# Attention on one core: probabilities as the stationary operand of the second matmul, in an order written by hand

## The chip, the cores and the metric

One NeuronCore of a Trainium2 chip runs the whole kernel. The metric is the device time of one execution in microseconds (us), the median over runs. TensorE does the matmuls and transposes (its weight loads, PEld, overlap them), ScalarE (ACT) the exponentials, VectorE (DVE) copies and arithmetic, GpSimd (POOL) casts and fills, SyncE (SP) issues transfers.

## The reference

```python
# q, k, v: (8, 8, 512, 64) float32: batch, heads, sequence, dim
scores = einsum('bhqd,bhkd->bhqk', q, k) / sqrt(64)
scores = scores - scores.max(axis=-1, keepdims=True)
attn = exp(scores)
attn = attn / attn.sum(axis=-1, keepdims=True)
return einsum('bhqk,bhkd->bhqd', attn, v)
```

There are 64 heads, each with a 512 x 512 matrix of scores. Neither kernel subtracts the maximum: both take the exponential of the scaled scores as they are and divide at the end by the sum over the keys.

## The kernel before

Heads are taken in 32 pairs, four to a batch entry. The 512 rows of a head lie on the 128 partitions four to a partition, so that a partition's four rows are neighbours in memory; chunk i (of `NI` = 4) is the i-th row of every partition. One pair goes through these stages.

- **Loads.** GpSimd's queue loads q and k of a batch entry at a time (`batch_load`, L49 and L54) and v head by head (L77), and the transfers turn fp32 into fp16 on their way. v lies in `vp` with a 65th column of ones (L75), so that the second matmul also gives the sum of the exponentials.
- **Transposes of q and k.** VectorE places the two heads of the pair side by side in `qkp` (L84, L88). TensorE transposes the eight 128 x 128 blocks into one bank of PSUM (L95, L96), and VectorE copies them out as `tqk` (L98). Head A then has its 64 dims on partitions 0 to 63, head B on 64 to 127.
- **Scores.** A matmul of 64 rows gives 128 keys (on partitions) by 512 queries (L110). A score tile holds two key chunks of one head, 128 x 1024 in fp32, two banks; there are two such tiles. ScalarE takes the exponential of a whole tile into fp16 `pt` (L118): four per pair, 128 in all.
- **Second matmul.** v with its ones is the stationary operand (128 x 65), 512 columns of `pt` stream past it, and four chunks add up into `ot`, 65 x 512: dims and sum on partitions, queries along the row (L131).
- **Output.** VectorE copies `ot` to SBUF (L140), TensorE transposes it back in four blocks per head, in fp32 (L148), and VectorE takes the reciprocal of the sum (L153) and multiplies (L154). SyncE stores 256 KB per pair (L161).

The order on each engine is the scheduler's of the tile framework: it interleaves the stages of neighbouring pairs by its own priorities, so the order in the text below is not the order on an engine. Buffers of a pool go round (`bufs`), and an instruction that writes one waits for the last reader of its former content.

Of the kernel before, what the change touches and what calls it, by code (L numbers as in the profile page):

```python
# [8 lines left out]
FP32 = mybir.dt.float32  # L9
FP16 = mybir.dt.float16  # L10

EXP = mybir.ActivationFunctionType.Exp
# [3 lines left out]
@with_exitstack  # L16
def kernel(
    ctx: ExitStack,
    tc: tile.TileContext,
    q: bass.AP,  # L20
    k: bass.AP,
    v: bass.AP,
    out: bass.AP,
):
    nc = tc.nc
    B, H, S, D = q.shape
    P = 128
    NI = S // P
    assert NI == 4 and D == 64 and S == 512
    scale = float(D) ** -0.5  # L30

    n_pairs = (B * H) // 2
    ppb = H // 2

    cpool = ctx.enter_context(tc.tile_pool(name="att_const", bufs=1))
    bpool = ctx.enter_context(tc.tile_pool(name="att_batch", bufs=2))
    apool = ctx.enter_context(tc.tile_pool(name="att_a", bufs=4))
    ppool = ctx.enter_context(tc.tile_pool(name="att_pair", bufs=3))
    hpool = ctx.enter_context(tc.tile_pool(name="att_head", bufs=4))
    opool = ctx.enter_context(tc.tile_pool(name="att_out", bufs=3))  # L40
    pspool = ctx.enter_context(tc.tile_pool(name="att_psum", bufs=1, space=bass.MemoryType.PSUM))

    bt = {}
    ident16 = None
    ident32 = None

    def batch_load(b):
        q16 = bpool.tile([P, H, NI * D], FP16, tag="q16", name=f"q16_{b}")
        nc.gpsimd.dma_start(  # L49
            out=q16.rearrange("p h (i d) -> p h i d", d=D),  # L50
            in_=q[b].rearrange("h (p i) d -> p h i d", i=NI),
        )
        k16 = bpool.tile([P, H, NI * D], FP16, tag="k16", name=f"k16_{b}")
        nc.gpsimd.dma_start(  # L54
            out=k16.rearrange("p h (i d) -> p h i d", d=D),
            in_=k[b].rearrange("h (p i) d -> p h i d", i=NI),
        )
        bt[b] = (q16, k16)

    batch_load(0)  # L60
    ident16 = cpool.tile([P, P], FP16, name="ident16")
    make_identity(nc, ident16)
    ident32 = cpool.tile([P, P], FP32, name="ident32")
    make_identity(nc, ident32)

    for g in range(n_pairs):
        b = g // ppb
        gl = g % ppb
        hA = 2 * gl
        if gl == 0 and b + 1 < B:  # L70
            batch_load(b + 1)
        q16, k16 = bt[b]

        vp = apool.tile([P, 2, NI, D + 1], FP16, tag="vp", name=f"vp_{g}")
        nc.gpsimd.memset(vp[:, :, :, D : D + 1], 1.0)  # L75
        for h01 in range(2):
            nc.gpsimd.dma_start(  # L77
                out=vp[:, h01, :, 0:D],
                in_=v[b, hA + h01].rearrange("(p i) d -> p i d", i=NI),
            )  # L80

        qkp = apool.tile([P, 2, NI, P], FP16, tag="qkp", name=f"qkp_{g}")
        for h01 in range(2):
            nc.vector.tensor_copy(  # L84
                out=qkp[:, 0, :, 64 * h01 : 64 * h01 + 64],
                in_=q16[:, hA + h01, :].rearrange("p (i d) -> p i d", d=D),
            )
            nc.vector.tensor_copy(  # L88
                out=qkp[:, 1, :, 64 * h01 : 64 * h01 + 64],
                in_=k16[:, hA + h01, :].rearrange("p (i d) -> p i d", d=D),  # L90
            )

        tqk_ps = pspool.tile([P, 2, NI, P], FP16, tag="ps_tqk", bufs=1, name=f"tqkps_{g}")
        for i in range(NI):
            nc.tensor.transpose(tqk_ps[:, 0, i, :], qkp[:, 0, i, :], ident16)  # L95
            nc.tensor.transpose(tqk_ps[:, 1, i, :], qkp[:, 1, i, :], ident16)  # L96
        tqk = ppool.tile([P, 2, S], FP16, tag="tqk", name=f"tqk_{g}")
        nc.vector.tensor_copy(out=tqk[:, :, :], in_=tqk_ps[:, :, :, :])  # L98

        pt = [hpool.tile([P, NI, S], FP16, tag="pt", name=f"pt_{g}_{h}") for h in range(2)]  # L100
        for half in range(2):
            st_ps = [
                pspool.tile([P, 2, S], FP32, tag="ps_st", bufs=2, name=f"st_{g}_{h01}_{half}")
                for h01 in range(2)
            ]
            for cc in range(2):
                c = 2 * half + cc
                for h01 in range(2):
                    po = 64 * h01
                    nc.tensor.matmul(  # L110
                        st_ps[h01][:, cc, :],
                        tqk[po : po + 64, 1, c * P : (c + 1) * P],
                        tqk[po : po + 64, 0, :],
                        start=True,
                        stop=True,
                    )
            for h01 in range(2):
                nc.scalar.activation(  # L118
                    out=pt[h01][:, 2 * half : 2 * half + 2, :],
                    in_=st_ps[h01][:, :, :],  # L120
                    func=EXP,
                    scale=scale,
                )

        ot_ps = [
            pspool.tile([P, S], FP32, tag="ps_ot", bufs=2, name=f"ot_{g}_{h01}")
            for h01 in range(2)
        ]
        for h01 in range(2):
            for c in range(NI):  # L130
                nc.tensor.matmul(  # L131
                    ot_ps[h01][0 : D + 1, :],
                    vp[:, h01, c, :],
                    pt[h01][:, c, :],
                    start=(c == 0),
                    stop=(c == NI - 1),
                )
        ot_sb = opool.tile([P, 2, S], FP32, tag="ot_sb", name=f"otsb_{g}")
        for h01 in range(2):
            nc.vector.tensor_copy(out=ot_sb[0 : D + 1, h01, :], in_=ot_ps[h01][0 : D + 1, :])  # L140

        out_sb = opool.tile([P, 2, NI, D], FP32, tag="out_sb", name=f"outsb_{g}")
        rcp = opool.tile([P, 2, NI], FP32, tag="rcp", name=f"rcp_{g}")
        for h01 in range(2):
            op_ps = pspool.tile([P, NI, D + 1], FP32, tag="ps_outp", bufs=1,
                                name=f"outp_{g}_{h01}")
            for c in range(NI):
                nc.tensor.transpose(  # L148
                    op_ps[:, c, :],
                    ot_sb[0 : D + 1, h01, c * P : (c + 1) * P],  # L150
                    ident32[0 : D + 1, 0 : D + 1],
                )
            nc.vector.reciprocal(out=rcp[:, h01, :], in_=op_ps[:, :, D : D + 1])  # L153
            nc.vector.tensor_tensor(  # L154
                out=out_sb[:, h01, :, :],
                in0=op_ps[:, :, 0:D],
                in1=rcp[:, h01, :].broadcast_to([P, NI, D]),
                op=AluOp.mult,
            )

        nc.sync.dma_start(  # L161
            out=out[b, hA : hA + 2].rearrange("h (p i) d -> p h (i d)", i=NI),
            in_=out_sb[:, :, :, :],
        )


# [28 lines left out]
```

## Time and profile before

| | |
|---|---|
| time, median of 3 runs | 191.35 us (190.75 to 191.9) |
| span of the profiled execution, its own time from the first to the last instruction | 189.0 us |
| TensorE matmul busy | 166.8 us (88%), 1024 instructions |
| ScalarE busy | 125.2 us (66%) |
| VectorE busy | 115.1 us (61%) |
| GpSimd busy | 66.5 us (35%) |
| granted TensorE clock, mean | 0.998 |
| HBM read, written | 25.17 MB, 8.39 MB |

The span is what the profiler saw of one execution; the median is of other executions of the same kernel, 2.35 us longer. A matmul's busy time counts the whole of its way through the array, so matmuls that follow each other overlap, and a busy TensorE is not one at its peak.

### The profile page before, as it was taken

Reading aid. Unit: us, or ns where it says so; the run is one execution under the profiler, and the core shown is the slowest. Engines: PE = TensorE matmul, PEld = TensorE weight load, DVE = VectorE, ACT = ScalarE, POOL = GpSimd, SP = SyncE. Lnnn points to the kernel's source line nnn. Section 1 sums busy time; section 2 is a strip of 40 time slices with the busy share of each in tenths; the row PEclk is TensorE's granted clock in tenths of the full one; section 3 lists DMA queues with packets and bytes.
Section 4 is the critical chain, followed back from the end, with each engine's and each line's share of the span. In section 5 each row is a group of like instructions: output and inputs, shape, how many; then the busy total and the mean of one; then the engine's idle time right before and its main releaser. Section 6 shows DMA issues by size and latency. Waiting matters only on the chain.

```text
span 189.0 us, 2952 instructions
## 1 busy us (share of the span) xinstructions
PE 166.8 (88%) x1024; PEld 74.9 (40%) x1024; DVE 115.1 (61%) x352; ACT 125.2 (66%) x129; POOL 66.5 (35%) x120
## 2 busy tenths in 40 slices
PE   0057999999999999999999999999999999999980
PEld 0033433434444343544353443434353443434330
DVE  0255455675859486666759585766757594656462
ACT  2014388688786868686886868686877868686860
POOL 7482643423453335413543336304133333300000
PEclk9999999999999999999999999999999999999999
DMA  3999999965599578995699478996555463631111
GB/s 42 191 182 183 129 156 189 179 87 77 65 147 196 80 91 111 182 170 83 86 143 188 74 91 126 179 149 87 83 83 76 34 90 67 87 69 59 55 57 55
DMA packets 59150, 21.16 MB, mean 112 GB/s; under 512 B 34560, under 2 KB 59136, under 8 KB 59136
## 3 DMA queue, kind: packets, MB, share of 16 engines
q0 software_dynamic: 50432, 12.59, 70.2%
q1 hardware_dynamic: 8704, 8.39, 12.8%
q8 instruction: 8, 0.13, 0.3%
q14 instruction: 6, 0.05, 0.1%
HBM read 25.17 MB, written 8.39 MB: 178 GB/s over the span
## 4 chain that ended last, share of the span: by engine, by line
PE 68%; DVE 11%; ACT 9%; DMA 6%; issue 2%; POOL 2%; ACTq 1%; POOLq 0%
PE st L110 31%; PE ot L131 31%; ACT pt L118 9%; DMA k<-in_k_dram 6%; DVE otsb L140 5%; DVE tqk L98 5%; PE outp L148 4%; PE tqkps L95 1%; POOL q L49 1%; ACTq L190 0%; POOL k L54 0%; DVE outsb L154 0%; DVE qkp L88 0%; POOL ident masks.py:199 0%; PE tqkps L96 0%
## 5 line engine op out<-in xcount | busy, mean ns | idle before, releaser
L118 ACT ACTIVATE pt<-st 128x1024 f16<-128x1024 f32 x128 | 124.0, 1024 | 56.8 <-PE st L110 56.8
L131 PE MATMUL ot<-pt,vp 128*65 128x512 f16 x256 | 73.4, 390 | 0.3 <-ACT pt L118 0.3
L140 DVE COPY otsb<-ot 65x512 f32<-65x512 f32 x64 | 43.8, 685 | 43.5 <-PE ot L131 43.5
L110 PE MATMUL st<-tqk 64*128 64x512 f16 x256 | 65.6, 386 | 3.6 <-DVE tqk L98 0.8
L77 POOL DMA_DIRECT2D vp<-in_v_dram x64 | 47.2, 743 | 14.4 <-POOL vp L75 9.6
L131 PEld LDWEIGHTS <-vp 128*65 128x65 f16 x256 | 21.9, 111 | 41.5 <-issue 33.9
L148 PEld LDWEIGHTS outp<-ident,otsb 65*128 65x128 f32 x256 | 23.4, 141 | 17.8 <-DVE otsb L140 9.3
L148 PE MATMUL outp<-ident,otsb 65*128 65x65 f32 x256 | 27.4, 229 | 3.2 <-DVE outsb L154 1.4
L75 POOL MEMSET vp<- 128x8 f16 x32 | 4.0, 139 | 70.6 <-PE ot L131 70.6
L95 PE MATMUL tqkps<-ident,qkp 128*128 128x128 f16 x128 | 21.0, 231 | 8.7 <-DVE qkp L84 7.6
L154 DVE TENSOR_TENSOR outsb<-outp,rcp 128x256 f32<-128x256 f32 x64 | 27.0, 422 | 1.3
L110 PEld LDWEIGHTS <-tqk 64*128 64x128 f16 x256 | 13.3, 94 | 25.7 <-issue 16.6
L96 PE MATMUL tqkps<-ident,qkp 128*128 128x128 f16 x128 | 20.9, 230 | 2.8 <-DVE qkp L88 2.8
L98 DVE COPY tqk<-tqkps 128x1024 f16<-128x1024 f16 x32 | 21.4, 670 | 0.5 <-PE tqkps L96 0.5
L84 DVE COPY qkp<-q 128x256 f16<-128x256 f16 x64 | 15.6, 256 | 8.4 <-DMA q<-in_q_dram 8.4
L153 DVE RECIPROCAL rcp<-outp 128x4 f32<-128x4 f32 x64 | 11.2, 175 | 14.5 <-PE outp L148 14.2
L95 PEld LDWEIGHTS <-qkp 128*128 128x128 f16 x128 | 12.8, 102 | 18.3 <-issue 7.6
L88 DVE COPY qkp<-k 128x256 f16<-128x256 f16 x64 | 16.4, 275 | 2.7 <-DMA k<-in_k_dram 2.7
L96 PEld LDWEIGHTS <-qkp 128*128 128x128 f16 x128 | 13.2, 103 | 6.9 <-DVE qkp L88 2.9
L49 POOL DMA_DIRECT2D q<-in_q_dram x8 | 7.2, 902 | 12.6 <-DVE qkp L88 9.2
L54 POOL DMA_DIRECT2D k<-in_k_dram x8 | 7.1, 892 | 0.1
L118 ACT ACT_TABLE_LOAD x1 | 1.3, 1283 | 0.7 <-PEq L179 0.7
(6 smaller groups left out, 1.3 us busy)
## 6 DMA issues: line engine op xcount, KB each, us to landing
out_dram<-outsb SPq DMA_DIRECT2D x32, 256.0 KB, 2.4
q<-in_q_dram POOLq DMA_DIRECT2D x8, 512.0 KB, 6.6
k<-in_k_dram POOLq DMA_DIRECT2D x8, 512.0 KB, 8.2
vp<-in_v_dram POOLq DMA_DIRECT2D x64, 64.0 KB, 3.1
```

What stands on the lines that cost most here:

```text
L77: nc.gpsimd.dma_start(out=vp[:, h01, :, 0:D], in_=v[b, hA + h01].rearrange("(p i) d -> p i d", i=NI),)
L84: nc.vector.tensor_copy(out=qkp[:, 0, :, 64 * h01 : 64 * h01 + 64], in_=q16[:, hA + h01, :].rearrange("p (i d) -> p i d", d=D),)
L88: nc.vector.tensor_copy(out=qkp[:, 1, :, 64 * h01 : 64 * h01 + 64], in_=k16[:, hA + h01, :].rearrange("p (i d) -> p i d", d=D),)
L95: nc.tensor.transpose(tqk_ps[:, 0, i, :], qkp[:, 0, i, :], ident16)
L96: nc.tensor.transpose(tqk_ps[:, 1, i, :], qkp[:, 1, i, :], ident16)
L98: nc.vector.tensor_copy(out=tqk[:, :, :], in_=tqk_ps[:, :, :, :])
L110: nc.tensor.matmul(st_ps[h01][:, cc, :], tqk[po : po + 64, 1, c * P : (c + 1) * P], tqk[po : po + 64, 0, :], start=True, stop=True,)
L118: nc.scalar.activation(out=pt[h01][:, 2 * half : 2 * half + 2, :], in_=st_ps[h01][:, :, :], func=EXP, scale=scale,)
L131: nc.tensor.matmul(ot_ps[h01][0 : D + 1, :], vp[:, h01, c, :], pt[h01][:, c, :], start=(c == 0), stop=(c == NI - 1),)
L140: nc.vector.tensor_copy(out=ot_sb[0 : D + 1, h01, :], in_=ot_ps[h01][0 : D + 1, :])
L148: nc.tensor.transpose(op_ps[:, c, :], ot_sb[0 : D + 1, h01, c * P : (c + 1) * P], ident32[0 : D + 1, 0 : D + 1],)
L154: nc.vector.tensor_tensor(out=out_sb[:, h01, :, :], in0=op_ps[:, :, 0:D], in1=rcp[:, h01, :].broadcast_to([P, NI, D]), op=AluOp.mult,)
```

## The change

The second matmul is turned round: a 128 x 128 block of the exponentials (128 keys by 128 queries) is the stationary operand and the 65 columns of v with its ones stream past it (`weigh`). The result has queries on partitions at once, so the copy of `ot` and the transposes of the output go. One pair has 32 such matmuls instead of eight of 512 columns and eight transposes.

A score tile holds one key chunk of both heads instead of two chunks of one head; a step is one tile, four steps to a pair, 128 in all. q, k and v of a pair come as fp32 in three transfers of 256 KB on SyncE's queue, and GpSimd casts them to fp16. The ones beside v are set once in four standing buffers. The order is written out (`manual_schedule`): in step t ScalarE does the exponential of t, and TensorE the scores of t+1, the weighing of t-1 and up to three transposes of the pair two ahead. Loads run five pairs ahead and casts two. A first small exponential stands ahead of the loop. Banks of PSUM: four for the score tiles, three for the results, one for the transposes.

```python
    def load(g):
        ...
        for nm, x in (("q", q), ("k", k), ("v", v)):
            r = lpool.tile([P, 2, NI * D], FP32, tag=f"{nm}32", name=f"{nm}32_{g}")
            nc.sync.dma_start(out=r, in_=src(x, g))
    def cast(g):
        ...
        q32, k32, v32 = raw.pop(g)
        qk = xpool.tile([P, 2, NI, P], FP16, tag="qk", name=f"qk_{g}")
        for n, r in enumerate((q32, k32)):
            nc.gpsimd.tensor_copy(
                out=qk[:, n].rearrange("p i (h d) -> p i h d", d=D),
                in_=r.rearrange("p h (i d) -> p i h d", d=D),
            )
        nc.gpsimd.tensor_copy(
            out=vps[g % NV][:, :, :, 0:D],
            in_=v32.rearrange("p h (i d) -> p h i d", d=D),
        )
    def transpose(g, lo, hi):
        ...
        if lo == 0:
            tps[g] = pspool.tile([P, 2, NI, P], FP16, tag="ps_t", bufs=1, name=f"tps_{g}")
        for n in range(lo, hi):
            nc.tensor.transpose(tps[g][:, n // NI, n % NI, :], halves[g][:, n // NI, n % NI, :], ident)
        if hi == 2 * NI:
            tqk[g] = xpool.tile([P, 2, S], FP16, tag="tqk", name=f"tqk_{g}")
            nc.vector.tensor_copy(out=tqk[g], in_=tps[g])
    def scores(t):
        ...
        st[t] = pspool.tile([P, 2, S], FP32, tag="ps_st", bufs=2, name=f"st_{t}")
        for h in range(2):
            po = D * h
            nc.tensor.matmul(
                st[t][:, h, :],
                tqk[g][po : po + D, 1, c * P : (c + 1) * P],
                tqk[g][po : po + D, 0, :],
                start=True,
                stop=True,
            )
    def softmax(t):
        pt[t] = ppool.tile([P, 2, S], FP16, tag="pt", name=f"pt_{t}")
        nc.scalar.activation(out=pt[t], in_=st.pop(t), func=EXP, scale=scale)
    def weigh(t):
        ...
                pspool.tile([P, NI, W], FP32, tag="ps_o", bufs=3, name=f"o_{g}_{h}")
                for h in range(2)
        ...
        for h in range(2):
            for i in range(NI):
                nc.tensor.matmul(
                    ops[g][h][:, i, :],
                    pt[t][:, h, i * P : (i + 1) * P],
                    vps[g % NV][:, h, c, :],
                    start=(c == 0 and i == 0),
                    stop=(c == NI - 1),
                    skip_group_check=True,
                )
        ...
        if c == NI - 1:
            finish(g)
    def finish(g):
        ...
        for h in range(2):
            o = ops[g][h]
            nc.vector.reciprocal(out=rcp[:, h, :], in_=o[:, :, D : D + 1])
            nc.vector.tensor_tensor(
                out=o_sb[:, h],
                in0=o[:, :, 0:D],
                in1=rcp[:, h, :].broadcast_to([P, NI, D]),
                op=AluOp.mult,
            )
        nc.sync.dma_start(
        ...
    AHEAD = 5
    with tc.manual_schedule():
        load(0)
        load(1)
        ...
        for g in range(2, AHEAD):
            load(g)
        cast(0)
        cast(1)
        transpose(0, 0, 2 * NI)
        scores(0)
        transpose(1, 0, 2 * NI)
        for t in range(n_steps):
            g, c = divmod(t, NI)
            if c == 0:
                cast(g + 2)
                load(g + AHEAD)
            softmax(t)
            scores(t + 1)
            if t > 0:
                weigh(t - 1)
            if c < NI - 1:
                transpose(g + 2, 3 * c, min(3 * c + 3, 2 * NI))
        weigh(n_steps - 1)
```

Pools for loads have six buffers, for `qk` and `tqk` three, for `pt` six.

## Rows read from the trace of the kernel before

**Rows 1.** The chain of work that ended last, by engine, share of the span.
```profile
PE 68%; DVE 11%; ACT 9%; DMA 6%; issue 2%; POOL 2%; ACTq 1%; POOLq 0%
```
**Rows 2.** Windows, steady stretch: us, busy (xinstructions) of each engine, clock, DMA.
```profile
22.00:182.00 160.00, 155.02 (x966) 69.41 (x966) 105.62 (x314) 119.16 (x124) 53.88 (x94) 1.00 0.80 109
```
**Rows 3.** Groups of instructions: count, busy us, mean ns, idle before and its releasers.
```profile
L118 ACT ACTIVATE pt<-st 128x1024 f16<-128x1024 f32 x128 | 124.0, 1024 | 56.8 <-PE st L110 56.8
...
L110 PE MATMUL st<-tqk 64*128 64x512 f16 x256 | 65.6, 386 | 3.6 <-DVE tqk L98 0.8 <-ACT pt L118 0.2
...
L148 PE MATMUL outp<-ident,otsb 65*128 65x65 f32 x256 | 27.4, 229 | 3.2 <-DVE outsb L154 1.4
L154 DVE TENSOR_TENSOR outsb<-outp,rcp 128x256 f32<-128x256 f32 x64 | 27.0, 422 | 1.3
L148 PEld LDWEIGHTS outp<-ident,otsb 65*128 65x128 f32 x256 | 23.4, 141 | 17.8 <-DVE otsb L140 9.3 <-issue 3.9 <-PE outp L148 1.1
...
L110 PEld LDWEIGHTS <-tqk 64*128 64x128 f16 x256 | 13.3, 94 | 25.7 <-issue 16.6 <-DVE tqk L98 4.9
...
L153 DVE RECIPROCAL rcp<-outp 128x4 f32<-128x4 f32 x64 | 11.2, 175 | 14.5 <-PE outp L148 14.2
...
L75 POOL MEMSET vp<- 128x8 f16 x32 | 4.0, 139 | 70.6 <-PE ot L131 70.6
...
masks.py:199 POOL TENSOR_SCALAR_AFFINE_SELECT ident<-ident 128x128 f16<-128x128 f16 x1 | 0.3, 324 | 0.0
...
masks.py:197 POOL MEMSET ident<- 128x128 f16 x1 | 0.2, 243 | 0.0
```
**Rows 4.** Timeline of ScalarE, two stretches without a gap: start, length in us.
```profile
90.46 3.86 ACT L118 ACTIVATE pt<-st 128x1024 f16<-128x1024 f32 x4 [1.87 <-PE st L110]
...
96.21 2.85 ACT L118 ACTIVATE pt<-st 128x1024 f16<-128x1024 f32 x3 [0.31 <-PE st L110]
```
**Rows 5.** Timeline of TensorE's matmuls between 89 and 96 us.
```profile
89.76 0.61 PE L110 MATMUL st<-tqk 64*128 64x512 f16 x4
...
90.37 0.22 PE L96 MATMUL tqkps<-ident,qkp 128*128 128x128 f16 x1
...
90.65 0.22 PE L95 MATMUL tqkps<-ident,qkp 128*128 128x128 f16 x1
...
94.18 0.60 PE L110 MATMUL st<-tqk 64*128 64x512 f16 x2
...
94.71 0.62 PE L131 MATMUL ot<-pt,vp 128*65 128x512 f16 x2
...
95.17 0.41 PE L148 MATMUL outp<-ident,otsb 65*128 65x65 f32 x4
```
**Rows 6.** Timeline of TensorE's weight loads in the same stretch.
```profile
90.97 0.32 PEld L148 LDWEIGHTS outp<-ident,otsb 65*128 65x128 f32 x4 [0.28 <-issue]
...
94.18 0.11 PEld L110 LDWEIGHTS <-tqk 64*128 64x128 f16 x2 [0.41 <-issue]
```
**Rows 7.** Timeline of the start: copies of k, first scores, first exponential, weight loads.
```profile
10.21 1.55 DVE L88 COPY qkp<-k 128x256 f16<-128x256 f16 x8 [1.87 <-DMA k<-in_k_dram]
...
12.35 1.03 PE L110 MATMUL st<-tqk 64*128 64x512 f16 x4 [0.79 <-DVE tqk L98]
...
13.42 1.94 ACT L118 ACTIVATE pt<-st 128x1024 f16<-128x1024 f32 x2 [11.40 <-PE st L110]
...
20.62 0.18 PEld L131 LDWEIGHTS <-vp 128*65 128x65 f16 x1 [0.25 <-issue]
21.02 0.54 PEld L131 LDWEIGHTS <-vp 128*65 128x65 f16 x3 [0.22 <-issue]
```
**Rows 8.** SyncE's transfers: share of 16 engines' span; count, KB, median us to landing.
```profile
q1 hardware_dynamic: 8704, 8.39, 12.8%
...
out_dram<-outsb SPq DMA_DIRECT2D x32, 256.0 KB, 2.4
```
**Rows 9.** Timeline of the end: the last product on VectorE.
```profile
185.56 0.42 DVE L154 TENSOR_TENSOR outsb<-outp,rcp 128x256 f32<-128x256 f32 x1
```

More of the change, by code (lines that the diff above doesn't have):

```diff
@@ L40 @@
+    xpool = ctx.enter_context(tc.tile_pool(name="att_x", bufs=3))
+    ppool = ctx.enter_context(tc.tile_pool(name="att_p", bufs=6))
     opool = ctx.enter_context(tc.tile_pool(name="att_out", bufs=3))
     pspool = ctx.enter_context(tc.tile_pool(name="att_psum", bufs=1, space=bass.MemoryType.PSUM))
[L43 to L51, printed above, removed]
-        )
[L53 to L79, printed above, removed]
-            )
[L82 to L104, printed above, removed]
-            ]
[L106 to L122, printed above, removed]
-                )
[L125 to L142, printed above, removed]
-        rcp = opool.tile([P, 2, NI], FP32, tag="rcp", name=f"rcp_{g}")
[L144 to L153, printed above, removed]
@@ new lines, in src @@
+    def src(x, g):
+        b, h = g // ppb, 2 * (g % ppb)
+        return x[b, h : h + 2].rearrange("h (p i) d -> p h (i d)", i=NI)
+    raw = {}
+    def load(g):
+        if g >= n_pairs:
+            return
+        t = []
+        for nm, x in (("q", q), ("k", k), ("v", v)):
+            r = lpool.tile([P, 2, NI * D], FP32, tag=f"{nm}32", name=f"{nm}32_{g}")
+            nc.sync.dma_start(out=r, in_=src(x, g))
+            t.append(r)
+        raw[g] = t
+    vps = [cpool.tile([P, 2, NI, W], FP16, name=f"vp{n}") for n in range(NV)]
@@ new lines @@
+    halves = {}
+    def cast(g):
+        if g >= n_pairs:
+            return
+        q32, k32, v32 = raw.pop(g)
[4 more added lines that the diff above has]
+                in_=r.rearrange("p h (i d) -> p i h d", d=D),
+            )
+        nc.gpsimd.tensor_copy(
+            out=vps[g % NV][:, :, :, 0:D],
+            in_=v32.rearrange("p h (i d) -> p h i d", d=D),
+        )
+        halves[g] = qk
@@ new lines @@
+    st, pt, ops = {}, {}, {}
+    n_steps = n_pairs * NI
+    def scores(t):
+        if t >= n_steps:
+            return
+        g, c = divmod(t, NI)
+        st[t] = pspool.tile([P, 2, S], FP32, tag="ps_st", bufs=2, name=f"st_{t}")
+        for h in range(2):
+            po = D * h
+            nc.tensor.matmul(
+                st[t][:, h, :],
+                tqk[g][po : po + D, 1, c * P : (c + 1) * P],
+                tqk[g][po : po + D, 0, :],
+                start=True,
+                stop=True,
+            )
@@ new lines, in softmax @@
+    def softmax(t):
+        pt[t] = ppool.tile([P, 2, S], FP16, tag="pt", name=f"pt_{t}")
+        nc.scalar.activation(out=pt[t], in_=st.pop(t), func=EXP, scale=scale)
+    def weigh(t):
+        g, c = divmod(t, NI)
+        if c == 0:
+            ops[g] = [
+                pspool.tile([P, NI, W], FP32, tag="ps_o", bufs=3, name=f"o_{g}_{h}")
+                for h in range(2)
+            ]
+        for h in range(2):
+            for i in range(NI):
+                nc.tensor.matmul(
+                    ops[g][h][:, i, :],
+                    pt[t][:, h, i * P : (i + 1) * P],
+                    vps[g % NV][:, h, c, :],
+                    start=(c == 0 and i == 0),
+                    stop=(c == NI - 1),
+                    skip_group_check=True,
+                )
+        del pt[t]
+        if c == NI - 1:
+            finish(g)
@@ L162 @@
             out=out[b, hA : hA + 2].rearrange("h (p i) d -> p h (i d)", i=NI),
-            in_=out_sb[:, :, :, :],
+            in_=o_sb,
         )
+        del ops[g]
+    AHEAD = 5
+    with tc.manual_schedule():
+        load(0)
+        load(1)
+        ident = cpool.tile([P, P], FP16, name="ident")
+        make_identity(nc, ident)
+        for n in range(NV):
+            nc.vector.memset(vps[n][:, :, :, D:W], 1.0)
+        warm = cpool.tile([P, 1], FP32, name="warm")
+        nc.vector.memset(warm, 0.0)
+        nc.scalar.activation(out=warm, in_=warm, func=EXP, scale=scale)
+        for g in range(2, AHEAD):
[6 more added lines that the diff above has]
+        for t in range(n_steps):
+            g, c = divmod(t, NI)
+            if c == 0:
+                cast(g + 2)
[7 more added lines that the diff above has]
+        weigh(n_steps - 1)
 _INS = ['q', 'k', 'v']
```

15 lines of the change are left out of this document (8 added, 7 removed).

## The prediction

> **What bounds the kernel now.** I read the chain of work that ended last first: two thirds of the span lie on TensorE, 9% on ScalarE [rows 1]. Then the steady stretch from 22 to 182 us: TensorE is busy for 155.0 of 160 us, ScalarE for 119.2 (124 exponentials), the rest of ScalarE's time is idle, and the groups of instructions say whom it waits for: TensorE's score matmuls, 56.8 us in all [rows 2, 3]. So TensorE sets the pace, one exponential per 160/124 = 1.29 us, 1.4 times what an exponential itself needs. That need is in ScalarE's timeline: three in a row take 2.85 us with 1.024 for one, so the pitch is (2.85 - 1.02)/2 = 0.913 us; four in a row take 3.86, a pitch of 0.947, the last pair of which still waited for TensorE [rows 3, 4]. 128 exponentials of the same size stay in the new kernel. Whatever TensorE gives back, the time can't fall under 127 x 0.913 + 1.02 = 117.0 us plus a head and a tail.
>
> TensorE's timeline shows what its pieces cost when they follow each other [rows 5]. Four score matmuls of alternating heads take 0.61 us, two of the same head 0.60: with one matmul 0.386 long [rows 3], the four start in two couples 0.61 - 0.386 = 0.22 us apart, so two heads, on rows 0 to 63 and 64 to 127 of the array, run as one. Transposes of 128 columns start (90.65 - 90.37)/5 = 0.056 us apart. The four output transposes (65 columns, fp32) take 0.41 with 0.229 for one: a pitch of 0.060. And of two score matmuls of one head the second starts at 94.18 + 0.21 = 94.39, the next weighing matmul at 94.71: 0.32 us where 0.22 would do, so 0.1 is lost at a change between half-height and full-height operands.
>
> **The change part by part**, per step (one exponential, a quarter of a pair of heads).
> *Scores.* Each step issues the two heads side by side, always a couple: 0.22 us.
> *Second matmul.* The eight of 512 columns per pair and the eight output transposes go, as do VectorE's copies for these. In their place stand 32 of 65 columns per pair, eight per step, each with its own 128-column weight load. No row shows that operation. From below, 65 columns at the transposes' rate: 65/128 x 0.056 = 0.028. From above, the output transposes, the same 128 loaded and 65 streamed columns, but in fp32: 0.060. What differs is the weight load: in fp32 four take 0.32 with 0.141 for one, 0.060 apart, so it was the load that set that pitch; two fp16 loads of 128 columns take 0.11 with 0.094 for one, 0.016 apart [rows 3, 6]. I take load and stream one after the other, 0.016 + 0.028 = 0.044, between the ends: eight make 0.35 us (0.22 to 0.48).
> *Input transposes.* Eight per pair as before, two per step on average: 0.11 us.
> *Changes of height.* Scores, then the rest, in every step: two, 0.2 us.
> TensorE's sum is 0.22 + 0.35 + 0.11 + 0.20 = 0.88 us per step (0.75 to 1.01), under ScalarE's 0.913 by a hair. The two meet where the new matmul costs 0.048.
>
> A rule of the Trainium skill speaks against this sum: "TensorE: Matmul & The Clock Gate", section "Back-to-back issue gap", gives a sustained stream of weight loads with matmuls of 128 columns some 81 ns each. The transposes here, the same form, go at 56 ns [rows 5], so the trace doesn't agree for short bursts; no run here shows a long one. By the Trainium skill a step would cost an estimated 0.22 + 10 x 0.081 + 0.2 = 1.23 us; by the rows it is 0.88.
>
> *Order.* The exponential of step t waits for its scores alone; scores(t+2) wait for exponential t, for there are two score tiles. From that end it is about 0.39 (a score matmul) and twice some 0.05 of signalling (13.42 against 12.35 + 1.03 [rows 7]) until the next exponential may start, some 0.5, and the exponential t+1 between them covers 0.9. So TensorE may be 0.4 us late without ScalarE seeing it; three transposes in one step (0.06 over the mean) are hidden by that. Behind scores(t+1) on TensorE stand the weighing of t-1, whose exponential is done when the scores may start, and transposes two pairs ahead. At a pair's end VectorE has two reciprocals and two products, 2 x (0.175 + 0.422) = 1.2 us [rows 3], and the copy of the transposes that it makes now too, in a pair of 3.65. The second head's weighing in the next pair takes the bank that the first product sets free, about 0.7 us after the last weighing; a step's scores and four weighings come before it. I cost that at nothing; uncovered it would be some 0.3 per pair, 10 us.
> *Loads.* GpSimd's transfers go; SyncE issues 96 loads of 256 KB in rows of 1 KB, the form of the stores. A store's share of the DMA engines is 12.8% of 189.0 us over 32 = 0.76 us and it lands in 2.4 [rows 8]; 128 transfers make 97 us of a span near 132. Loads are asked for three pairs (11 us) before their cast, so the landing is hidden after the start. Behind a waiting store on SyncE stand loads of a pair six ahead: no cost.
> *Casts.* GpSimd gets three per pair, 512 elements each. Nearest rows: filling 8 columns takes 0.139, filling 128 takes 0.243, masking 128 takes 0.324 [rows 3]. From above, four maskings: 1.30. From below, the fill's growth per column: 0.139 + 504 x 0.104/120 = 0.58. I take 0.85, as a cast reads and writes like the masking but pays the fixed part once; that is 2.6 us per pair, under ScalarE's 3.65. It decides from 1.22. On GpSimd nothing else is queued but one identity at the start, and who waits for a late cast is TensorE's transposes, two pairs ahead.
>
> **Head.** Before, the last copy of k ends at 10.21 + 1.55 = 11.76 and the first exponential starts at 13.42, 1.66 later [rows 7]. After: if SyncE issues from about 0.7 (an estimate; no transfer of it stands at the start), q lands at 0.7 + 2.4 = 3.1 [rows 8], k at 3.9; two casts end at 4.8; with 1.7 for transposes, copy and scores, 6.5. I take 7.0 (5.5 to 9).
> **The slow start.** Before 21 us the same work takes double: four score matmuls 1.03 instead of 0.61, and the weight loads of the weighing matmuls, one per matmul, stand 0.40 apart at 20.62 and 21.02, while the three from 21.02 all lie within 0.54 [rows 7]: that is the 1.2 GHz level, though the granted clock is given as 1.00. TensorE had been at work since the scores at 12.35, with short breaks. At that level a new step costs about 0.43 + 0.2 + 8 x 0.08 + 0.22 = 1.5 us; I count five such steps, which lose 5 x 0.6 = 3 us (1 to 5).
> **Tail.** Before, the last product ends at 185.56 + 0.42 = 185.98, 3.0 before the end [rows 9]. After the last exponential come eight weighings and their latency (0.7), the four operations of VectorE (1.25) and these 3.0: 5.0 us.
>
> Sum: 7.0 + 3.0 + 117.0 + 5.0 = 132.0 us of span, 57 less than 189.0. The median of the runs, 191.35, is 2.35 above the profiled span; with the same distance the forecast is **134.4 us**.
>
> **The rivals.**
> *TensorE stays the bound* (24%). The margin of 0.03 per step is smaller than my doubt on the weighing. At 0.060 each a step takes 1.01: 128 x 1.01 = 129.3, and 129.3 + 15.0 + 2.35 = 146.6 us. For it: the nearest whole row is the fp32 one. Against it: its load, not its stream, sets that pitch.
> *Weight loads that nothing hides* (4%). If a long stream of loads with short matmuls paid each load's whole 0.094 [rows 3], a step would be 0.22 + 8 x 0.094 + 0.11 + 0.2 = 1.28 us, and 128 x 1.28 + 17.35 = 181 us. Against it: the transposes' 0.056 is less than one load. The Trainium skill's rule on the stream of weight loads (the section named above) points this way; the trace does not.
> *GpSimd becomes the bound* (8%). At 1.30 per cast a pair takes 3.9 us: 32 x 3.9 = 124.8, starting at 3.1, then 6 us for the last pair and the tail of 5: 138.9 + 2.35 = 141 us. At 1.6 it is 170.
> *The clock falls* (6%), the one that can end slower. If TensorE goes back to the 1.2 GHz level, a step has 0.43 for scores, 0.22 transposes, 0.2 changes and eight weighings at twice 0.028 to 0.060: 1.3 to 1.8 us, a time of 184 to 248 us. It is slower than before from 0.064 per weighing (128 x 1.36 + 17.4 = 191.5). For it: the new matmuls stream few columns each. Against it: at the low level TensorE would never be idle, and the clock rose before in just such a state [rows 7] and stayed at 1.00 [rows 2].
> *A wait I overlooked* (3%), for instance the late bank above: 145 us.
>
> **How the numbers follow.** ScalarE as the bound has 55%: its own range is, from below, 5.5 + 1 + 117.0 + 4.7 + 2.35 = 130.5, less 1.3 for a pitch of 0.903 as the quickest couple may have had, 129; from above, with 0.947 throughout, 9 + 5 + 121.3 + 5.3 + 2.35 = 143. The range over the cases reaches from 129 to 150: it takes in TensorE at 0.060 and GpSimd to 1.38 per cast, and leaves out the falling clock, the unhidden loads, slower casts and some luck below. About 0.5% can be told from no change. Faster has 0.95, the slow end of the falling clock and of a mishap like it 0.04, the same 0.01.
>
> **What would show it.** Right: exponentials 0.91 us apart in the steady stretch with ScalarE waiting for almost nothing, the chain on ScalarE instead of TensorE; score matmuls in couples; weighings 0.03 to 0.05 apart; casts near 0.85; the first exponential near 7 us. Wrong: ScalarE's idle time still put down to the score matmuls; weighings 0.06 or more apart; transposes waiting for casts; matmuls at double length after the first 20 us.

## The result, and the profile after

The changed kernel takes **133.71 us** (median of 4 runs, 133.68 to 134.23) against 191.17 us for the kernel before on the same chip (190.75 to 191.9): a ratio of 0.6995, 95% interval 0.6971 to 0.7018. The forecast was 134.4, with a range of 129 to 150. The profiled execution took 133.69 us, its span 131.8 (forecast 132.0), and its mean granted clock is 0.99.

The page of the changed kernel: span, busy time by engine, granted clock over 40 slices, SyncE's queue (share of the 16 DMA engines), the chain by engine and by line, groups of instructions, transfers. They answer to [rows 1, 3, 8].

```profile
span 131.8 us, 3961 instructions
PE 112.5 (85%) x1536; PEld 71.2 (54%) x1536; DVE 58.1 (44%) x165; ACT 119.4 (91%) x130; POOL 56.9 (43%) x102
PEclk9999999999999999999999999999999999999995
q1 hardware_dynamic: 34816, 33.56, 79.3%
ACT 72%; issue 10%; PE 8%; DMA 4%; SPq 2%; DVE 1%; POOL 0%
L112 ACT ACTIVATE pt<-st 128x1024 f16<-128x1024 f32 x128 | 117.9, 1197 | 7.1 <-PE st L102 7.0
L123 PE MATMUL o<-vp,pt 128*128 128x65 f16 x1024 | 54.2, 196 | 0.8 <-ACT pt L112 0.7
L123 PEld LDWEIGHTS <-pt 128*128 128x128 f16 x1024 | 38.5, 98 | 30.1 <-issue 29.0
L69 POOL CAST qk<-q 128x512 f16<-128x512 f32 x32 | 19.7, 616 | 3.2 <-DMA q<-in_q_dram 3.0
q<-in_q_dram SPq DMA_DIRECT2D x32, 256.0 KB, 4.1
```

The chain has moved from TensorE (68% before) to ScalarE (72%). ScalarE waits 7.0 us for scores where it waited 56.8, and the waits list these 7.0 us as four waits, the longest 4.9. The mean of 1197 ns is not what an exponential costs: 128 of that length would be 153 us, and 117.9 are busy, so the rows of queued exponentials overlap. The pitch, below, is the cost. The windows of a steady stretch answer to [rows 2]; columns as there.

```profile
25.00:125.00 100.00, 92.62 (x1303) 59.54 (x1303) 48.90 (x137) 100.00 (x110) 42.25 (x73) 1.00 0.80 254
```

ScalarE is busy for 100.00 of 100 us. That alone doesn't make it the bound: in e8, below, it is busy for 79.07 of 80 us while TensorE sets the pace. What speaks for it is its pitch, 0.917 us (worked out below), close to the 0.913 of exponentials in a row before, and that TensorE waits for it; e1 and e2 test it. TensorE's "busy" 92.62 is not its need either: the timeline of its matmuls, which answers to [rows 5], shows where it waits.

```profile
60.35 0.39 PE L102 MATMUL st<-tqk 64*128 64x512 f16 x2
60.67 0.42 PE L123 MATMUL o<-vp,pt 128*128 128x65 f16 x8
61.27 0.39 PE L102 MATMUL st<-tqk 64*128 64x512 f16 x2 [0.18 <-ACT pt L112]
61.59 0.42 PE L123 MATMUL o<-vp,pt 128*128 128x65 f16 x8
61.85 0.33 PE L87 MATMUL tps<-ident,qk 128*128 128x128 f16 x3
62.18 0.39 PE L102 MATMUL st<-tqk 64*128 64x512 f16 x2
```

Two score matmuls end 0.39 us after they start, the length of one (387 ns): a couple. Eight weighings take 0.42 with 0.196 for one, so they start (0.42 - 0.196)/7 = 0.032 us apart, and what follows them starts 0.26 after they do. Between the scores and the weighing lie 0.32 us where the couple needs 0.22: the change of height costs 0.1. At 61.27 TensorE has been idle for 0.18 us and waited for ScalarE.

The start and the end, from the timeline (a row counts neighbours of one kind and gives the first start and the time to the last end). They answer to [rows 4, 7, 9].

```profile
3.64 0.61 POOL L69 CAST qk<-q 128x512 f16<-128x512 f32 x1 [2.34 <-DMA q<-in_q_dram]
...
7.09 1.02 ACT L112 ACTIVATE pt<-st 128x1024 f16<-128x1024 f32 x1 [4.86 <-PE st L102]
...
9.15 1.02 ACT L112 ACTIVATE pt<-st 128x1024 f16<-128x1024 f32 x1 [1.04 <-PE st L102]
10.87 1.02 ACT L112 ACTIVATE pt<-st 128x1024 f16<-128x1024 f32 x1 [0.70 <-PE st L102]
11.63 0.61 PE L102 MATMUL st<-tqk 64*128 64x512 f16 x2
...
13.66 0.39 PE L102 MATMUL st<-tqk 64*128 64x512 f16 x2
...
125.94 1.29 ACT L112 ACTIVATE pt<-st 128x1024 f16<-128x1024 f32 x1
```

The first three exponentials stand alone, each waiting for scores; the fourth starts at 12.28. A couple takes 0.61 until 11.63 and 0.39 from 13.66: the 1.2 and the 2.4 GHz level. From the fourth exponential to the last, 124 pitches lie in 125.94 - 12.28 = 113.66 us, 0.917 each.

### The profile page after: what moved, and what is told of

It reads as the page before. It is cut to its first block, busy times and chain, and to the rows that moved or that the text cites. A ratio compares the mean times of both kernels' runs of the same rounds, so it can differ in the third digit from the quotient of the medians.

```text
span 131.8 us, 3961 instructions
## 1 busy us (share of the span) xinstructions
PE 112.5 (85%) x1536; PEld 71.2 (54%) x1536; DVE 58.1 (44%) x165; ACT 119.4 (91%) x130; POOL 56.9 (43%) x102
## 3 DMA queue, kind: packets, MB, share of 16 engines
q1 hardware_dynamic: 34816, 33.56, 79.3%
## 4 chain that ended last, share of the span: by engine, by line
ACT 72%; issue 10%; PE 8%; DMA 4%; SPq 2%; DVE 1%; POOL 0%
ACT pt L112 72%; DMA q<-in_q_dram 4%; PE st L102 4%; PE o L123 3%; SPq L56 2%; PE tps L87 1%; DVE osb L142 1%; POOL qk L69 0%; DVE rcp L141 0%
## 5 line engine op out<-in xcount | busy, mean ns | idle before, releaser
L112 ACT ACTIVATE pt<-st 128x1024 f16<-128x1024 f32 x128 | 117.9, 1197 | 7.1 <-PE st L102 7.0
L102 PE MATMUL st<-tqk 64*128 64x512 f16 x256 | 51.1, 387 | 9.0 <-ACT pt L112 6.0
L123 PE MATMUL o<-vp,pt 128*128 128x65 f16 x1024 | 54.2, 196 | 0.8 <-ACT pt L112 0.7
L123 PEld LDWEIGHTS <-pt 128*128 128x128 f16 x1024 | 38.5, 98 | 30.1 <-issue 29.0
L73 POOL CAST vp<-v 128x512 f16<-128x512 f32 x32 | 19.8, 619 | 52.8 <-PE o L123 51.1
L90 DVE COPY tqk<-tps 128x1024 f16<-128x1024 f16 x32 | 22.1, 692 | 36.0 <-PE tps L87 36.0
L87 PE MATMUL tps<-ident,qk 128*128 128x128 f16 x256 | 31.0, 227 | 5.4 <-POOL qk L69 5.2
L142 DVE TENSOR_TENSOR osb<-o,rcp 128x256 f32<-128x256 f32 x64 | 27.1, 424 | 2.5 <-DMA out_dram<-osb 0.3
L69 POOL CAST qk<-q 128x512 f16<-128x512 f32 x32 | 19.7, 616 | 3.2 <-DMA q<-in_q_dram 3.0
L87 PEld LDWEIGHTS <-qk 128*128 128x128 f16 x256 | 16.5, 101 | 7.0 <-POOL qk L69 7.0
L69 POOL CAST qk<-k 128x512 f16<-128x512 f32 x32 | 19.7, 617 | 0.5
```

The lines of the kernel that those rows point to most:

```text
L69: nc.gpsimd.tensor_copy(out=qk[:, n].rearrange("p i (h d) -> p i h d", d=D), in_=r.rearrange("p h (i d) -> p i h d", d=D),)
L73: nc.gpsimd.tensor_copy(out=vps[g % NV][:, :, :, 0:D], in_=v32.rearrange("p h (i d) -> p h i d", d=D),)
L87: nc.tensor.transpose(tps[g][:, n // NI, n % NI, :], halves[g][:, n // NI, n % NI, :], ident)
L90: nc.vector.tensor_copy(out=tqk[g], in_=tps[g])
L102: nc.tensor.matmul(st[t][:, h, :], tqk[g][po : po + D, 1, c * P : (c + 1) * P], tqk[g][po : po + D, 0, :], start=True, stop=True,)
L112: nc.scalar.activation(out=pt[t], in_=st.pop(t), func=EXP, scale=scale)
```

## The experiments

The theory behind the runs: ScalarE sets the pace (0.917 us per step), TensorE needs about 0.8 and hides, and the gain came from the turned matmul. Rivals: TensorE or the transfers are still what decides, or the gain came from the order or the loads. Diffs are against the changed kernel; ratios are to the kernel before, where the changed kernel has 0.6995.

### Half of each exponential left out (e1_half_exp)

The exponential covers the first head's scores alone and both heads are weighed with it, so the output isn't attention's; TensorE's work stays.

```diff
-        pt[t] = ppool.tile([P, 2, S], FP16, tag="pt", name=f"pt_{t}")
-        nc.scalar.activation(out=pt[t], in_=st.pop(t), func=EXP, scale=scale)
+        pt[t] = ppool.tile([P, S], FP16, tag="pt", name=f"pt_{t}")
+        nc.scalar.activation(out=pt[t], in_=st.pop(t)[:, 0, :], func=EXP, scale=scale)
```

> The exponential covers only the first head's half of each score tile (128 x 512 instead of 128 x 1024), and both heads are weighed with it: half of ScalarE's work is left out, TensorE's, VectorE's, GpSimd's and the transfers stay as they are. Theory (ScalarE sets the pace, TensorE needs some 0.79 us per step: 0.22 scores, 8 x 0.032 weighing, 0.11 transposes, 0.2 changes of height): the step falls from 0.917 to about 0.80 us and the time to 128 x 0.80 + 16 = 118 us, with TensorE on the chain. Rival (TensorE is the bound already and ScalarE only keeps up with it): 133 us, unchanged. Second rival (the transfers, 79% of 131.8 us, come next): near 120 us too, but with casts and transposes waiting for loads.

119.82 us, ratio 0.6266 (0.6237 to 0.6294). The chain by engine:

```profile
PE 85%; DMA 5%; DVE 3%; SPq 2%; issue 1%; POOL 1%; ACT 1%; ACTq 0%
```

The steady windows:

```profile
25.00:105.00 80.00, 79.85 (x1200) 47.95 (x1198) 45.06 (x125) 59.12 (x101) 42.49 (x73) 1.00 0.97 312
```

With ScalarE relieved the chain goes back to TensorE, and a step takes 80/100 = 0.80 us (some 100 exponentials in 80 us). So ScalarE did set the pace, and TensorE stands 0.12 us behind it. The transfers' share rises to 0.97 in that stretch, and the chain still has only 5% of DMA, so the second rival, the transfers, isn't what holds this run.

### Every weighing matmul twice (e2_weigh_twice)

```diff
-            for i in range(NI):
+            for n in range(2 * NI):
+                i = n % NI
```

> Each of the 32 weighing matmuls per pair is issued twice (both the sums and the divisor double). Theory: TensorE's step grows by 8 x 0.032 = 0.26 us from 0.79 to 1.05, passes ScalarE's 0.917 and becomes the pace: 128 x 1.05 + 16 = 150 us, of which 0.13 per step is hidden in TensorE's idle time. Rival (TensorE has no idle time to give): 133.7 + 128 x 0.26 = 167 us. Rival (long streams of loads with short matmuls run slower than short ones, 0.06 or more each): 0.79 + 8 x 0.06 = 1.27 per step or more, 179 us or more.

147.86 us, 0.7725 (0.7694 to 0.7756); the chain is 69% TensorE. Its timeline:

```profile
60.23 0.66 PE L124 MATMUL o<-vp,pt 128*128 128x65 f16 x16
```

Sixteen take 0.66 us: with 0.195 for one they start (0.66 - 0.195)/15 = 0.031 us apart, in a stream twice as long as the kernel's. The step is the sum of the pieces, 0.22 + 16 x 0.031 + 0.11 + 0.20 = 1.03; in ScalarE's timeline 64 exponentials go from 44.16 to 110.03 us, 1.03 each.

### Score tiles of one head (e3_one_head_tiles)

Two key chunks of one head in a tile, as before the change, with the second matmul and the order of the change.

```diff
-        for h in range(2):
-            po = D * h
+        h, po = c % 2, D * (c % 2)
+        for n in range(2):
+            kc = 2 * (c // 2) + n
             nc.tensor.matmul(
-                st[t][:, h, :],
-                tqk[g][po : po + D, 1, c * P : (c + 1) * P],
+                st[t][:, n, :],
+                tqk[g][po : po + D, 1, kc * P : (kc + 1) * P],
...
```

> A score tile holds two key chunks of one head again, so its two matmuls use the same rows of the array; everything else, the written order too, is that of the changed kernel. Theory (the couples run as one and save 0.215 us per step): TensorE's step becomes 0.79 + 0.215 = 1.0 us, over ScalarE's 0.917: 128 x 1.0 + 16 = 144 us. Rival (ScalarE's pace hides it): 133.7 us, unchanged.

**233.85 us** (four executions, 233.66 to 234.31), 1.2236 (1.2199 to 1.2274): neither the theory nor the rival. The page's busy times:

```profile
PE 222.7 (96%) x1536; PEld 93.2 (40%) x1536; DVE 61.1 (26%) x165; ACT 132.6 (57%) x130; POOL 56.7 (24%) x102
```

The timeline of TensorE:

```profile
100.86 1.03 PE L103 MATMUL st<-tqk 64*128 64x512 f16 x2
101.82 0.62 PE L126 MATMUL o<-vp,pt 128*128 128x65 f16 x8
102.25 0.51 PE L87 MATMUL tps<-ident,qk 128*128 128x128 f16 x3
102.70 0.61 PE L103 MATMUL st<-tqk 64*128 64x512 f16 x1
```

The mean granted clock is listed as 1.000, but 0.62 for eight weighings and 0.51 for three transposes are the durations that the changed kernel has only at its start (0.62 at 10.76, 0.51 at 11.19). At 100 us TensorE still runs at the 1.2 GHz level, and it is busy for 96% of the span. Is it the level that costs 100 us, or the couples that are gone? The next two runs ask.

### The same behind a burst of matmuls (e8_one_head_burst)

The kernel of e3 with 40 matmuls of full height and 512 columns ahead.

```diff
+        for n in range(40):
+            nc.tensor.matmul(fill_ps, ident, filler, start=True, stop=True)
```

> The kernel of the run with one head per score tile (233.9 us, all of it at matmul durations of the 1.2 GHz level) with a burst of 40 full matmuls of 512 columns ahead of everything, results unused. Theory (the level is lost again when the one-head stream takes over: its matmuls keep TensorE occupied but do not hold the clock): durations fall back after the burst, 234 + some 8 = 242 us. Rival (once up, a TensorE without pauses stays up): 144 + 8 = 152 us.

148.68 us, 0.7763 (0.7734 to 0.7792); one of its four executions, not in the ratio, took 239.19 us, about the time of e3, and its mean granted clock is listed as 0.535. The timeline of TensorE in one of the other three:

```profile
1.45 10.69 PE L167 MATMUL fill_ps<-filler,ident 128*128 128x512 f16 x40 [1.45 <-DVE filler L164]
...
60.67 0.60 PE L103 MATMUL st<-tqk 64*128 64x512 f16 x2
61.20 0.42 PE L126 MATMUL o<-vp,pt 128*128 128x65 f16 x8
```

Its steady windows:

```profile
25.00:105.00 80.00, 79.94 (x962) 38.72 (x960) 38.10 (x100) 79.07 (x81) 34.74 (x61) 1.00 0.84 264
```

The rival was right in three executions of four: once at 2.4 GHz, the same stream stayed there. So the clock made about 85 of e3's 100 us. Without couples two scores take 0.60 and a step 1.00 us (of the 81 exponentials in the window one is cut by its edges), 0.08 over the changed kernel's, which is 10 us in 128 steps. The other 5 are the start: the first exponential comes at 14.02, 6.9 us later, and the 2.4 us that the changed kernel loses behind its first one fall away.

### Scores of full height (e11_full_height_scores)

Each head's keys lie in a tile of 128 rows whose other half is zero, so that all scores use 128 rows: no couples, and no change of height. VectorE makes three copies for one.

```diff
-                tqk[g][po : po + D, 1, c * P : (c + 1) * P],
-                tqk[g][po : po + D, 0, :],
+                kz[g % 3][h][:, c * P : (c + 1) * P],
+                tqk[g],
...
```

> Scores with all 128 rows: the keys of each head lie in a tile whose other half is zero, the two heads' queries stream past it, so nothing runs as a couple (two times 0.216 us) and no height changes (0.2 us less). TensorE's step at 2.4 GHz: 0.43 + 0.26 + 0.11 = 0.80 us, as now, and the time 134 to 136 us. For the clock: theory (the one-head stream failed to raise it because half of the rows stood idle in turn): it rises within the first 20 us as in the changed kernel. Rival (without couples in the stream it doesn't rise): about 1.5 us per step, 208 us.

134.61 us, 0.7033 (0.7006 to 0.7061). The timeline of TensorE at the start, and two lines of a later step:

```profile
8.54 1.06 PE L107 MATMUL st<-tqk,kz 128*128 128x512 f16 x2
...
10.40 0.96 PE L107 MATMUL st<-tqk,kz 128*128 128x512 f16 x2
11.20 0.41 PE L128 MATMUL o<-vp,pt 128*128 128x65 f16 x8
...
11.61 0.59 PE L107 MATMUL st<-tqk,kz 128*128 128x512 f16 x2
...
60.37 0.59 PE L107 MATMUL st<-tqk,kz 128*128 128x512 f16 x2
...
60.80 0.40 PE L128 MATMUL o<-vp,pt 128*128 128x65 f16 x8
```

The scores go one behind the other, as in e3, and the level rises at 11 us. So being serial alone isn't what kept e3 down: in e3, with half-height serial scores, the clock didn't rise; in the changed kernel, with couples, and here, with full height, it did. From the scores at 60.37 to the weighing at 60.80 are 0.43 us, two matmuls at 0.21 to 0.22 each, so the 0.1 that was lost there at a change of height is gone. The couples are also worth little here: what they save, 0.6 - 0.39 = 0.2 us, is what two changes of height cost.

### The second matmul as before (e5_v_stationary, e9_v_stationary_scheduled)

v stationary again, with the copy of the result and the fp32 transposes back; in the written order, and in the scheduler's.

```diff
-            for i in range(NI):
-                nc.tensor.matmul(
-                    ops[g][h][:, i, :],
-                    pt[t][:, h, i * P : (i + 1) * P],
-                    vps[g % NV][:, h, c, :],
...
+            nc.tensor.matmul(
+                ops[g][h][0:W, :],
+                vps[g % NV][:, h, c, :],
+                pt[t][:, h, :],
...
```

> The second matmul as before (v with its ones stationary, 512 columns of probabilities streaming, the copy and the fp32 transposes of the output back), everything else as in the changed kernel. Theory (the turned matmul takes TensorE under ScalarE's pace): TensorE's step is 0.22 scores + 2 x 0.216 + 0.11 + 2 x 0.06 output transposes + 0.2 changes of height = 1.08 us, and the time 128 x 1.08 + 17 = 155 us. Rival (the gain came from the couples, the order and the loads, and the second matmul's form is hidden under ScalarE): within 2% of 133.7 us.

177.12 us, 0.9256 (0.9225 to 0.9287), far over the theory's number. The timeline at a pair's end shows why:

```profile
91.01 1.29 DVE L133 COPY otsb<-ot 65x512 f32<-65x512 f32 x2 [0.56 <-PE ot L122]
...
91.75 0.38 PE L122 MATMUL ot<-pt,vp 128*65 128x512 f16 x1
...
92.35 0.38 PE L122 MATMUL ot<-pt,vp 128*65 128x512 f16 x1 [0.22 <-DVE otsb L133]
```

The next pair's second head waits on TensorE for the second copy, and the scores behind it wait too; VectorE's copies are 24% of the chain. I put that down to my order for it and the two banks for the sums, not to the matmul; a third bank was not tried. Hence the same in the scheduler's order:

> The run with v stationary again, but in the order of the framework's scheduler instead of mine, in which the second head's sums waited at every pair's end for VectorE's copies of the two banks. Theory (177.1 us was 1.08 us per step of TensorE and 0.2 of that wait): with the wait spread, 1.08 per step, 150 to 160 us. Rival (the copies and output transposes cost this form the waits in any order): 170 us or more.

163.52 us, 0.8543 (0.8515 to 0.8571), between the numbers of the two theories. The chain is 77% TensorE and still 14% VectorE's copies, and ScalarE waits for scores again:

```profile
ACT pt L112 <- PE st L102: 26.2, 64, 4.7
```

With the kernel that follows (e4) as its partner in the same order, the turned matmul is worth 163.52 - 132.92 = 31 us, the copies and output transposes that go with it and the waits for them included, and all that is left of the change, from 191.17 to 163.52, some 28.

### The scheduler's order (e4_scheduler_order)

```diff
-    with tc.manual_schedule():
+    if True:
```

> The same instructions without the written order: the framework's scheduler puts them in its own. Theory (the work per engine decides, and 0.4 us of lateness is hidden): within 3% of 133.7 us. Rival (the written order is part of the gain: the scheduler breaks the couples or lets the weighing wait): 140 us or more, with ScalarE waiting for scores.

132.92 us, 0.696 (0.6925 to 0.6995): no difference to the changed kernel that can be told. The chain is 75% ScalarE. The written order brings nothing here, which fits the 0.12 us per step that TensorE has to spare.

### The loads as before (e6_old_loads)

Loads that cast on their way on GpSimd's queue, q and k by batch entry, and VectorE placing the heads; no casts on GpSimd.

```diff
-        for nm, x in (("q", q), ("k", k), ("v", v)):
-            r = lpool.tile([P, 2, NI * D], FP32, tag=f"{nm}32", name=f"{nm}32_{g}")
-            nc.sync.dma_start(out=r, in_=src(x, g))
+        for nm, x in (("q", q), ("k", k)):
+            r = bpool.tile([P, H, NI * D], FP16, tag=f"{nm}16", name=f"{nm}16_{b}")
+            nc.gpsimd.dma_start(
...
```

> Loads as before (GpSimd's queue, fp32 to fp16 on the way, q and k by batch entry, v by head, VectorE placing the heads side by side), everything else as in the changed kernel. Theory A (the old transfers fill the DMA engines: 70.2% of 189.0 us for them and 24 us for the stores, 157 us): the time rises to 157 us or more, with transposes or weighings waiting for transfers. Theory B (their share was only high because they had the time; ScalarE stays the bound): 134 to 140 us, the start some 4 us later.

140.3 us, 0.7349 (0.7324 to 0.7374), just over what B expected. GpSimd's queue on the page:

```profile
q0 software_dynamic: 50432, 12.59, 97.2%
```

ScalarE's waits for scores (us, times, longest):

```profile
ACT pt L119 <- PE st L109: 13.2, 6, 10.4
```

Its first exponential in the timeline:

```profile
12.59 1.02 ACT L119 ACTIVATE pt<-st 128x1024 f16<-128x1024 f32 x1 [10.35 <-PE st L109]
```

That queue's packets take 97.2% of the engines' span, and ScalarE waits six times in the whole run, 13.2 us against 7.0. The first exponential comes 12.59 - 7.09 = 5.5 us later, nearly the whole of the 6.6 us that the loads are worth. In the steady part the old loads are hidden: from 25 to 125 us 110 exponentials run, as in the changed kernel.

### A better start (e7_better_head, e10_better_head_2, e12_better_head_3)

What is left is the start: 7.09 us, and another 12.28 - 7.09 - 3 x 0.917 = 2.4 until the exponentials follow each other. Three versions put q and k of two pairs ahead of v, let VectorE cast k of these, give TensorE nine matmuls of 512 columns to do, and issue the transposes of the next pairs later.

```diff
-        load(0)
-        load(1)
+        load(0, "qk")
+        load(1, "qk")
+        load(0, "v")
+        load(1, "v")
...
-            nc.gpsimd.tensor_copy(
+            (nc.vector if n and g < 2 else nc.gpsimd).tensor_copy(
...
+        for n in range(8):
+            nc.tensor.matmul(fill_ps, ident, filler, start=True, stop=True)
...
+        early = {0: (1, 0, 8), 3: (2, 0, 4), 4: (2, 4, 8), 6: (3, 0, 4), 7: (3, 4, 8)}
```

> The changed kernel with another start: q and k of two pairs loaded before v, VectorE casting k of these two, nine filler matmuls while TensorE waits for the first loads, and transposes of the next pairs issued later, behind scores that are ready. Theory (2.5 us are lost between the first and the fourth exponential, to transposes waiting for casts and to the 1.2 GHz level): first exponential at about 6.6 us, the next ones 0.917 apart, 131 us. Rival (the gaps only move to later steps): 133.7 us.

133.27 us, 0.6976 (0.6948 to 0.7005). The first exponential came at 8.36: on VectorE the copy of the transposes stood behind the cast of the second pair's k, which waited for its transfer. TensorE was idle for 1.94 us before the scores, and its granted clock was 0.50 from 9 to 12 us. The second version puts the first pair's transposes and copy ahead of that cast.

> The better start once more, with the transposes' copy of the first pair ahead of the second pair's casts on VectorE, which had held it up until 7.19 us. Theory: first exponential at about 6.6 us, the next ones without gaps, 1.7 us less than the last time: 131.5 us. Rival (TensorE falls to the 1.2 GHz level while it waits, and its slow steps let ScalarE wait): 133 us or more.

133.38 us, 0.6967 (0.6946 to 0.6988). ScalarE's timeline, and TensorE's transposes of the second pair:

```profile
6.75 1.94 ACT L114 ACTIVATE pt<-st 128x1024 f16<-128x1024 f32 x2 [4.51 <-PE st L104]
11.51 2.12 ACT L114 ACTIVATE pt<-st 128x1024 f16<-128x1024 f32 x2 [2.82 <-PE st L104]
9.89 1.04 PE L89 MATMUL tps<-ident,qk 128*128 128x128 f16 x8 [2.97 <-POOL qk L71]
```

The windows after that idle time; the third number from the end is the granted clock:

```profile
9.00:12.00 3.00, 2.11 (x20) 1.39 (x20) 0.69 (x1) 0.49 (x1) 2.85 (x6) 0.50 1.09 351
```

The first exponential is early now, but on GpSimd the second pair's q stood behind the first pair's v, whose transfer came at 8.66. TensorE waited 2.97 us for it and fell to half its clock. The third version casts that q first:

```diff
-        cast(0)
-        cast(1)
+        cast(0, "qk")
         transpose(0, 0, 2 * NI)
+        cast(1, "qk")
+        cast(0, "v")
+        cast(1, "v")
```

> The better start a third time: the first scores' copy ahead of VectorE's later casts as in the second, and on GpSimd q of pair 1 ahead of v of pair 0, which held it up until 8.66 us. Theory: first exponential at about 6.7 us and at most 1.5 us of gaps behind it, 131.5 to 132 us. Rival (the start is set by the landing of the first six transfers, 0.75 us each, and by slow steps after TensorE's wait, whatever the order): 133 to 134 us.

**130.77 us** (130.49 to 131.18, 5 runs), 0.6846 (0.6822 to 0.6869): 0.6846/0.6995 = 0.979, 2.1% under the changed kernel, and the intervals don't meet. It beats both kernels. The timeline:

```profile
6.81 10.19 ACT L116 ACTIVATE pt<-st 128x1024 f16<-128x1024 f32 x11 [4.58 <-PE st L106]
6.92 0.62 PE L91 MATMUL tps<-ident,qk 128*128 128x128 f16 x8
...
8.21 0.41 PE L127 MATMUL o<-vp,pt 128*128 128x65 f16 x8
```

From the first exponential at 6.81 on no pause shows, the first weighings have the durations of 2.4 GHz, and the granted clock is 1.00 in all windows. The gain, 2.9 us, is the 2.4 of the slow start and 0.3 of an earlier first exponential, and 0.2 that these don't explain. With the same nine matmuls and other orders e7 and e10 gained nothing that can be told; whether the order of e12 would do it without the matmuls, no run shows.

## Why the prediction was right, point by point

**The bound.** Its likeliest case (55%) held: the chain is on ScalarE, and e1 and e2 moved the bound to TensorE when ScalarE had less to do or TensorE more. The pitch is 0.917 where 0.913 was forecast.

**The weighing**, the term that decided between the two engines, was taken too dear: 0.044 forecast, 0.032 measured, near the lower bound of 0.028, which was worked out from the transposes' rate for 65 columns. The load, which was added to the stream (at 0.016, read from loads of 64 rows), doesn't show as a term of its own: one load takes 0.098 us, and eight matmuls with eight loads, or sixteen with sixteen in e2, still start 0.031 to 0.032 apart. That also answers the rival of loads that nothing hides (4%). TensorE's step is 0.22 + 8 x 0.032 + 0.11 + 0.20 = 0.79 instead of 0.88, and e1 shows 0.80. So the margin was 0.12 us per step instead of 0.03, and the rival that kept TensorE as the bound (24%) was never near. The rule of the Trainium skill, "TensorE: Matmul & The Clock Gate", section "Back-to-back issue gap", would have made a step 1.23 us by the estimate in the prediction, which put the figure for 128 columns on the matmuls of 65 too; the trace doesn't agree, with 0.80 us a step in e1 and 0.031 us apiece in e2's streams of sixteen. A long stream of 128 columns is in no run.

**Couples and changes of height** held: 0.39 for two scores, 0.1 lost at a change.

**Casts:** 0.85 forecast (0.58 to 1.30), 0.616 measured, near the bound by the fill's growth per column. GpSimd has 56.9 us of work, and is no bound.

**Loads:** landing takes 4.1 us in the median for q (k 4.4, v 4.7) where 2.4 was taken from the stores before, and loads and stores together are 79.3% of 131.8 = 104 us where 97 was forecast. Both are hidden, as argued. The first cast started at 3.64 instead of 3.1, and the first exponential at 7.09 instead of 7.0.

**The slow start** lost 2.4 us (3.0 forecast), and that the two are so near is in part luck. The forecast counted five steps at the 1.2 GHz level, 0.6 us each. The run has three late steps, which lose 1.14, 0.80 and 0.49 us (2.06, 1.72 and 1.41 less 0.917). In the third TensorE works without a pause, so 0.49 is what the level costs. The first two also hold TensorE's waits for GpSimd's casts, 0.20 us before the transposes at 7.24 and 0.68 before those at 9.78, for which the prediction had no term. In e12 the whole loss is gone.

**The tail:** the last exponential ends at 125.94 + 1.29 = 127.23, 4.6 us before the end (5.0 forecast). The late bank, costed at nothing, cost nothing: weighings waited 0.8 us in the whole run, 0.7 of it for exponentials.

**The sum** was right by parts that were off by little and partly cancelled: 0.09 later, 0.6 less of a slow start, 0.7 more of exponentials (127 x 0.0036, and the last one's row is 1.29 long instead of 1.02), 0.4 less of a tail. The distance of median and span is 133.71 - 131.8 = 1.9 instead of 2.35.

**What was argued wrongly** is the case against the falling clock (6%): that a TensorE which is never idle at the low level gets the high one back. In e3 it was busy for 96% of 232.5 us and never did. The chance was small for a reason that didn't hold, and as far as that argument goes it was luck that this rival stayed away: one edit nearer to the kernel before, this rival would have come true, at 233.85 us, inside the 184 to 248 that the prediction gave it.

**Where the gain came from.** The turned matmul brought 31 us (e9 against e4). The loads were worth 6.6 when undone alone (e6), the order nothing (e4), and the couples 10 us of steps at 2.4 GHz (e8), and without them, with the tiles of e3, the level itself was lost. These don't add up to 57 since each is hidden as long as another engine is the bound.

## What to carry to other kernels

Where an accumulation must be transposed back at its end, make the big operand the stationary one: a weight load of 128 columns under each matmul of 65 showed no cost of its own here (0.032 us for both), and two output copies and eight transposes per pair went. Cost each engine per step of the loop, and take the largest: what brings an engine under it is worth nothing more, as the written order shows, and the rest to gain is the start, where each queue's first instructions should stand in the order in which their transfers land. Look at matmul durations, not at the clock's row alone, for what level TensorE runs at.

## What the runs showed of the hardware that I had not expected

TensorE can stay at 1.2 GHz for a whole kernel though it hardly ever idles: in e3, 96% busy, eight weighings took 0.62 us at 100 us as at the start, against 0.42, and the granted clock is listed as 1.000 all the same. The execution of e8 that took 239.19 us has 0.535 listed, so the list can show such a run for what it is, but didn't in e3. The same stream behind 40 full matmuls ran at 2.4 GHz in three executions of four (147.74 to 148.7, and once 239.19); with full-height scores (e11) or couples (the changed kernel, busy for 2.32 us of the 3 from 9 to 12) it rose by itself at 11 to 13 us. Which property of the stream decides, and why one execution in four behaved otherwise, stays open: the runs differ in rows at work, in durations and in the share of each shape. The kernel before, too, has scores of one head one behind the other (two in 0.60 us [rows 5]) and ran at 2.4 GHz, beside a second matmul of another form, so such scores alone don't settle it.

In the other direction, TensorE's granted clock stood at 0.50 after idle stretches of 1.94 us (e7) and 2.97 us (e10) early in the kernel; in e12, with the same burst ahead and no wait over 0.6 us after it, it stayed at 1.00.

A stream of 65-column matmuls, each with its own load of 128 columns, goes at 0.031 us apiece (e2), faster than the transposes' 0.056 [rows 5]: with half as many streamed columns the time nearly halves, and no load shows as a term of its own.
